# Queued weight splits, redealt product banks and a shared decay-weight buffer in a two-layer hybrid encoder

## The chip, the cores and the metric

The kernel runs on one core of a Trainium2 chip. The metric is device time in microseconds, the median of several executions. A profiled execution gives a trace of every instruction; times in the text count from the start of its span. The core's engines work side by side, each through its own instructions in order: TensorE (PE; PEld is its weight load), VectorE (DVE), ScalarE (ACT), GpSimd (POOL) and SyncE (SP), which here only issues DMAs. POOL issues DMAs as well, among them DMAs that add their source to what the destination holds.

## What is computed

The reference runs two layers over 512 tokens of width 1024. Each layer is a token mixer (first a gated DeltaNet, GDN, then gated linear attention, GLA), a residual with LayerNorm, a squared-ReLU MLP of width 4096, and a residual with LayerNorm again:

```python
for i in range(DEPTH):
    m = _mixer_gdn(x, ...) if i % 2 == 0 else _mixer_gla(x, ...)
    x = _layernorm(DEEPNORM_ALPHA * x + m, ln1_g[i], ln1_b[i])
    x = _layernorm(DEEPNORM_ALPHA * x + _sq_relu_mlp(x, mlp_w1[i], mlp_w2[i]), ln2_g[i], ln2_b[i])

def _sq_relu_mlp(h, w1, w2):
    a = jax.nn.relu(jnp.matmul(h, w1))
    return jnp.matmul(a * a, w2)

def _mixer_gla(h, w_in, gate_w2, gate_b, norm_g, w_out):
    proj = jnp.matmul(h, w_in)                      # q, k, v, r and a rank-16 gate input per direction
    gate_logit = jnp.einsum('bsnr,nrk->bnsk', gl, gate_w2) + gate_b
    log_a = jax.nn.log_sigmoid(gate_logit) / B_TAU  # decay of each key channel, two directions
    ...
```

## The kernel before

Four stages follow one another on the one core: GDN, first MLP, GLA, second MLP. All large products are done to almost fp32 accuracy out of reduced-precision operands: every matrix is **split** into a high part (`hi`, a ScalarE copy that rounds) and a low part (`lo`, what is left, usually a VectorE subtraction), and `mm3` issues three matmuls for one: hi·hi, hi·lo and lo·hi (L119 to L121). So every weight tile goes through the same steps: a DMA from HBM on SP's queue into one of **three buffers** of the tag `wst` (`Ctx.dma`, L50), the ScalarE copy (L96) and the VectorE subtraction (L101) into `wh` and `wl`, of which there are three each. `split` has another form, `by_dma`: ScalarE writes hi and the negated source (L98), and a POOL DMA adds the source to it (L99); VectorE isn't used.

The instructions are traced in the order of the Python code, which is also their priority; a scheduler then places each on its engine's queue, when its own model of time says that its data and buffers are there. A later stage's instruction may so come to stand ahead of an earlier stage's. What is once placed on an engine runs in that order. Orders that are wanted are written by hand: `in_order` chains the instructions of an engine as traced, and `issue_after(ins)` puts what is traced within it behind `ins` on the same engine.

**The MLP.** `mlp` takes the 4096 hidden features in four groups of eight tiles. Group 0's features are computed plainly (`feature`, L334 and L335 are its ReLU and square). In the later groups, `Pair` computes two feature tiles over 512 tokens with seven half-size products instead of eight (Strassen's method, 128x256 each, twelve matmuls a product), into three accumulators X, Y and Z; X and Z lie in one PSUM bank and Y in another (tag `pj`, two banks). ScalarE copies or VectorE sums read them (L448 after product 1, L451 after product 2, L454, L457, L460, L463, then the ReLUs). The order of the products is 1, 2, 6, 5, 7, 3, 4. The scheduler treats a bank as a whole: a matmul into a bank waits for the read of its other half.

The second matrix is multiplied with the same method on the level of blocks: `second` runs seven products (1, 2, 5, 6, 7, 3, 4) for each group, interleaved with the next group's `Pair` products on TensorE, and `last` does it for the last group alone. `pair` splits an operand out of the hidden features (`ah`, `al`), `load` fetches a block of the second matrix (`w2r`, eight buffers), `split(i)` splits it (`w2h`, `w2l`), `plus` adds one block to another. In `last`, the order on POOL, ScalarE and VectorE is fixed up to product 3; after that come a4's `pair`, product 7 with the sums `full` (L584), the LayerNorm `norm` of token tiles 0 and 1 (on VectorE L224, L227, L233, L195 to L202, L238; on ScalarE the squares of L226 and the Ln and Exp of L193 and L194), and product 4, into which the transposes of those tiles are put (`turn`, `xpose`, L181, with the copies L184 and L185). The LayerNorms of tiles 2 and 3 come behind it.

**The GLA stage** begins with `proj_halves`: the gates' input (`gps`), then head 0's q (`pjq`) and k (`pjk`), for the first half of the tokens and then the second, with the transposes of tiles 2 and 3 in the middle of k's first half. Its weights are traced in this order: `gst` (split by `side_by_side`, L160 and L162), q, k, and, behind `proj_halves`, the decay weights `gate_w2` of the two directions: each into its own `wst` buffer `w2f`, a ScalarE copy of 96 rows (L793) and a VectorE subtraction in 32 of them (L794). Then the gates of head 0 follow (`gates`: a matmul `lg`, L864, five ScalarE steps, a VectorE sum, L866 to L872), and the levels of the decayed scores (`levels`, `scp`, L950, each fed by VectorE products such as `qh`, L961).

`behind(n)` puts n **units** of other matmul work in front of what follows on TensorE: one token tile of a quarter of v and r's depth (`vr`, six matmuls), a quarter of a q or k projection (`qk`, six matmuls) or a piece of the output projection. There are 104 units in all, and the calls ask for 8 ahead of the first level, 24 for each of the four heads and what is left at the end.

**The MLP's beginning.** The weights of features 0 to 2 are fetched ahead by the stage before, those of features 3 to 7 in `mlp`. At feature 5 the first blocks of the second matrix, (0, 0) and (0, 1), are loaded, at feature 6 block (1, 1), and there the first block is split and a1's pair made. `x_blocks` builds the sums of x that the `Pair` products need, in four of the eight `w2r` buffers, from feature 5 on.

Of the kernel before, what the change touches and what calls it, by code (L numbers as in the profile page):

```python
# [8 lines left out]
F32 = mybir.dt.float32  # L9
# [8 lines left out]
P = 128  # L18
S = 512
# [9 lines left out]
class Ctx:  # L29
# [55 lines left out]
    def split(self, src, shape, pool=None, by_dma=False):  # L85

        nc = self.nc
        if pool is None:
            hi = self.whl.tile(shape, F32R, name="wh", tag="wh")
            lo = self.whl.tile(shape, F32R, name="wl", tag="wl")  # L90
        else:
            pool, hi, lo, bufs = pool
            if pool:
                hi = pool.tile(shape, F32R, name=hi, tag=hi, bufs=bufs)
                lo = pool.tile(shape, F32R, name=lo, tag=lo, bufs=bufs)
        nc.scalar.copy(hi, src)  # L96
        if by_dma:
            nc.scalar.mul(lo, src, -1.0)  # L98
            nc.gpsimd.dma_start(lo, src, accum_op=ALU.add)  # L99
        else:  # L100
            nc.vector.tensor_tensor(lo, src, hi.bitcast(F32), ALU.subtract)  # L101
        return hi, lo

    def wcols(self, w, c0, n=P, pool=None):

        st = self.wst.tile([P, KT, n], F32, name="wst", tag="wst")
        self.dma(st, w[:, c0:c0 + n].rearrange("(k p) n -> p k n", p=P))
        return self.split(st, [P, KT, n], pool)

# [64 lines left out]
    def xpose(self, t, src, tags=("tp",)):  # L174

        nc = self.nc
        for q in range(2):
            ps = self.bank([P, 4, P], F32, name="tp", tag=tags[(2 * t + q) % len(tags)])
            for i in range(4):
                k = 4 * q + i  # L180
                nc.tensor.transpose(ps[:, i, :], src[:, k * P:(k + 1) * P], self.ident)  # L181
            hi = self.xth[:, 4 * q:4 * q + 4, t * P:(t + 1) * P]
            lo = self.xtl[:, 4 * q:4 * q + 4, t * P:(t + 1) * P]
            last = nc.scalar.copy(hi, ps)  # L184
            self.last_lo = nc.vector.tensor_tensor(lo, ps, hi.bitcast(F32), ALU.subtract)  # L185
        return last

    def rsqrt(self, out, x, n, eps, times=None):
# [4 lines left out]
        nc.scalar.activation(y, x, AF.Ln, bias=self.bias[eps])  # L193
        nc.scalar.activation(y, y, AF.Exp, scale=-0.5)  # L194
        nc.vector.tensor_tensor(t, y, y, ALU.mult)  # L195
# [18 lines left out]
    def layernorm(self, z, out, par, last=False, sums=None):  # L214
# [21 lines left out]
        for q in range(2):  # L236
            if True:
                nc.vector.scalar_tensor_tensor(out[q], out[q], rstd[:, 0:1], par[2 + q], ALU.mult, ALU.add)  # L238
            else:
# [69 lines left out]
def mlp(c, w1, w2, g, b, out=None, extra=None):  # L309
# [14 lines left out]
    with c.banks(pj=2, X=2, Y=2, Z=2), tc.tile_pool(name="mlp", bufs=2) as pool:  # L324
# [73 lines left out]
        class Pair:  # L398
# [41 lines left out]
            def products(self, h):  # L440
# [3 lines left out]
                l, r = slice(0, HT), slice(HT, S)  # L444
                xz, y = c.bank([P, 2, HT], F32, name="fxz", tag="pj"), c.bank([P, 2, HT], F32, name="fy", tag="pj")
                X, Z, Y = xz[:, 0, :], xz[:, 1, :], y[:, 0, :]
                self.mm(X, 1)
                A.copy(h0[:, l], X)  # L448
                yield
                self.mm(Z, 2, False)  # L450
                V.tensor_tensor(h0[:, l], h0[:, l], Z, ALU.add)  # L451
# [3 lines left out]
                yield  # L455
                self.mm(Y, 5)
                A.copy(h1[:, r], Y)  # L457
# [104 lines left out]
        def last(gi, h, a):  # L562
# [82 lines left out]

# [123 lines left out]
def gla(c, gc, w_in, gate_w2, w_out, ln_g, ln_b, w_next):  # L769
# [5 lines left out]
    with c.banks(ac=2, tp=2, pj=4), tc.tile_pool(name="gla", bufs=2) as pool:  # L775
# [10 lines left out]
        R = slice(0, 32), slice(32, 64), slice(64, 96)  # L786
        glr, w2r = [], []
        for d in range(2):
            w2f = c.wst.tile([96, S], F32, name="w2f", tag="wst")
            src = gate_w2[d]  # L790
            c.dma(w2f, bass.AP(src.tensor, src.offset, [[0, 6]] + [list(q) for q in src.ap]))
            t = pool.tile([96, S], F32R, name=f"w2r{d}", bufs=1)
            nc.scalar.copy(t, w2f)  # L793
            nc.vector.tensor_tensor(t[R[2], :], w2f[R[2], :], t[R[2], :].bitcast(F32), ALU.subtract)  # L794
            w2r.append(t)
            g = pool.tile([96, S], F32R, name=f"glr{d}", bufs=1)
# [11 lines left out]
        with c.in_order(mybir.EngineType.PE):  # L808
# [13 lines left out]

            behind(8)
            after = None
# [895 lines left out]
```

## Time and profile before

| | |
|---|---|
| median of 3 executions | 1362.85 us (1362.2 to 1363.65) |
| the profiled execution | 1365.3 us |
| its span | 1363.6 us |
| mean granted clock of TensorE | 0.991 of full |
| TensorE, VectorE, ScalarE, GpSimd busy | 97%, 80%, 58%, 9% of the span |
| matmuls | 8629 |
| DMA traffic | 153.16 MB, mean 112 GB/s |

In rows of the timeline stand the start and the duration in us, the engine, the line, the operation, what is written and read with shapes, and in brackets how long the engine stood idle before and what released it. Names are tiles of the program; several instructions of one kind in a row are merged (x2). The view of waits sums, for each pair of instructions, the time that the first one's engine stood idle for the second. The chain of waits follows the work that ended last back to the start.

### The profile page before, as it was taken

Reading aid. Unit: us, or ns where it says so; the run is one execution under the profiler, and the core shown is the slowest. Engines: PE = TensorE matmul, PEld = TensorE weight load, DVE = VectorE, ACT = ScalarE, POOL = GpSimd, SP = SyncE. Lnnn points to the kernel's source line nnn. Section 1 sums busy time; section 2 is a strip of 40 time slices with the busy share of each in tenths; the row PEclk is TensorE's granted clock in tenths of the full one; section 3 lists DMA queues with packets and bytes.
Section 4 is the critical chain, followed back from the end, with each engine's and each line's share of the span. In section 5 each row is a group of like instructions: output and inputs, shape, how many; then the busy total and the mean of one; then the engine's idle time right before and its main releaser. Section 6 shows DMA issues by size and latency. Waiting matters only on the chain.

```text
span 1363.6 us, 22194 instructions
## 1 busy us (share of the span) xinstructions
PE 1328.0 (97%) x8629; PEld 1128.2 (83%) x8629; DVE 1096.5 (80%) x1786; ACT 794.6 (58%) x1552; POOL 118.4 (9%) x169
## 2 busy tenths in 40 slices
PE   8999999999999999999998999999999999999996
PEld 8777777778777989889897878888889789898985
DVE  6687877788777878989887877967879678989888
ACT  3776568665743555666566555654445456566654
POOL 4000000000000910101101100000000001101010
PEclk9999999999999999999998999999999999999998
DMA  6221112110141684775647332212225576757555
GB/s 178 76 63 48 48 32 63 47 48 32 63 135 52 189 186 141 161 182 151 150 143 155 95 119 62 78 47 74 81 78 160 144 178 146 161 167 144 153 136 127
DMA packets 155532, 153.16 MB, mean 112 GB/s; under 512 B 7659, under 2 KB 122467, under 8 KB 155427
## 3 DMA queue, kind: packets, MB, share of 16 engines
q1 hardware_dynamic: 144355, 111.90, 27.8%
q0 software_dynamic: 11072, 39.86, 15.1%
q8 instruction: 67, 1.10, 0.3%
q14 instruction: 38, 0.31, 0.1%
HBM read 113.99 MB, written 2.10 MB: 85 GB/s over the span
## 4 chain that ended last, share of the span: by engine, by line
PE 75%; DVE 12%; ACT 8%; issue 2%; DMA 2%; DVEq 0%; SPq 0%; POOL 0%; ACTq 0%; POOLq 0%
PE fxz L119 3%; PE fxz L121 3%; PE fxz L120 3%; PE pjv L119 3%; PE pjv L120 3%; PE pjv L121 3%; PE pX L119 2%; PE pX L120 2%; PE pX L121 2%; PE pY L120 2%; PE scp L950 2%; PE pY L121 2%; PE op L1646 2%; PE pY L119 2%; PE pj L121 2%
## 5 line engine op out<-in xcount | busy, mean ns | idle before, releaser
L96 ACT CAST wh<-wst 128x1024 fp32r<-128x1024 f32 x150 | 157.2, 1048 | 164.9 <-PE pjz L120 41.0
L101 DVE TENSOR_TENSOR wl<-wst,wh 128x1024 fp32r<-128x1024 f32 x150 | 184.3, 1231 | 54.3 <-ACT wh L96 53.5
L101 DVE TENSOR_TENSOR w2l<-w2r,w2h 128x1024 fp32r<-128x1024 f32 x92 | 112.5, 1223 | 33.9 <-ACT w2h L96 33.7
L96 ACT CAST w2h<-w2r 128x1024 fp32r<-128x1024 f32 x94 | 98.4, 1047 | 60.0 <-PE pX L121 24.7
L364 POOL DMA_DIRECT2D w2r<-w2r x56 | 48.3, 892 | 512.0 <-DVE w2l L101 297.1
L96 ACT CAST ah<-h 128x1024 fp32r<-128x1024 f32 x56 | 58.8, 1050 | 53.1 <-PE pZ L120 19.6
L101 DVE TENSOR_TENSOR al<-h,ah 128x1024 fp32r<-128x1024 f32 x56 | 68.4, 1222 | 8.4 <-ACT ah L96 8.4
L119 PE MATMUL fxz<-xth,wh 128*128 128x256 f32 x264 | 74.8, 283 | 0.2 <-ACT h L448 0.2
L121 PE MATMUL fxz<-xth,wl 128*128 128x256 f32 x264 | 74.5, 282 | 0.0
L120 PE MATMUL fxz<-xtl,wh 128*128 128x256 f32 x264 | 74.5, 282 | 0.0
L413 DVE TENSOR_TENSOR wst<-wst 128x512 f32<-128x512 f32 x110 | 73.1, 683 | 0.2
L119 PE MATMUL pj<-xth,wh 128*128 128x256 f32 (+1 forms) x192 | 64.8, 339 | 2.3 <-ACT xth L184 1.4
L120 PE MATMUL pX<-w2l,ah 128*128 128x512 f32 x168 | 66.1, 394 | 0.0
L119 PE MATMUL pX<-w2h,ah 128*128 128x512 f32 x168 | 66.1, 393 | 0.0
L121 PE MATMUL pX<-w2h,al 128*128 128x512 f32 x168 | 65.7, 391 | 0.0
L120 PE MATMUL pj<-xtl,wh 128*128 128x256 f32 (+1 forms) x192 | 64.7, 337 | 0.0
L121 PE MATMUL pj<-xth,wl 128*128 128x256 f32 (+1 forms) x192 | 64.6, 337 | 0.0
L119 PE MATMUL pjv<-wh,xth 128*128 128x512 f32 x128 | 54.7, 428 | 0.0
L119 PEld LDWEIGHTS fxz<-xth,wh 128*128 128x128 f32 x264 | 50.1, 190 | 4.8 <-ACT h L448 1.5
L120 PEld LDWEIGHTS fxz<-xtl,wh 128*128 128x128 f32 x264 | 50.2, 190 | 2.4
L119 PE MATMUL fxz<-xh,wh 128*128 128x256 f32 x176 | 50.2, 285 | 1.6 <-DVE h L451 1.4
L121 PE MATMUL pjv<-wh,xtl 128*128 128x512 f32 x128 | 50.2, 392 | 0.0
(504 smaller groups left out, 4256.0 us busy)
## 6 DMA issues: line engine op xcount, KB each, us to landing
wst<-in_mlp_w SPq DMA_DIRECT2D x68, 512.0 KB, 5.1
w2r<-in_mlp_w SPq DMA_DIRECT2D x60, 512.0 KB, 4.3
w2r<-w2r POOLq DMA_DIRECT2D x56, 512.0 KB, 5.7
wst<-in_a_w_in SPq DMA_DIRECT2D x32, 512.0 KB, 4.1
wst<-in_b_w_in SPq DMA_DIRECT2D x32, 256.0 KB, 3.1
wst<-in_a_w_out SPq DMA_DIRECT2D x8, 512.0 KB, 3.9
wst<-in_b_w_in SPq DMA_DIRECT2D x8, 512.0 KB, 3.9
wst<-in_b_w_out SPq DMA_DIRECT2D x8, 512.0 KB, 3.7
```

The source lines that it names most:

```text
L96: nc.scalar.copy(hi, src)
L101: nc.vector.tensor_tensor(lo, src, hi.bitcast(F32), ALU.subtract)
L119: mm(ps, ah, bh, start=start, stop=False, **kw)
L120: mm(ps, ah, bl, start=False, stop=False, **kw)
L121: mm(ps, al, bh, start=False, stop=stop, **kw)
L364: nc.gpsimd.dma_start(blocks[a + (q,)], blocks[b + (q,)], accum_op=ALU.add)
L413: plus = lambda a, b: V.tensor_tensor(a, a, b, ALU.add)
L950: T.matmul(ps[:, n, :], kh[:, sl], qh[:, sl], start=True, stop=True)
L1646: T.matmul(op[:, n, :], l, r, start=i == 0, stop=i == len(mm) - 1)
```

## The change

It has five parts.

1. `split` and the LayerNorm keep hold of some of their instructions (`halves`: the copy and the subtraction of the latest plain split; `normed`: the Exp and the last VectorE step of the latest LayerNorm). `wcols` takes a list `late` of instructions behind which its split is queued. GLA's q weights are split behind the two halves of a4's pair in the MLP's `last`, GLA's k weights behind the second LayerNorm's Exp, and k's lo is made by a POOL DMA (`by_dma`).
2. In `products`, X has a bank for itself, and Y and Z share one.
3. The two directions' decay weights are loaded into one `wst` buffer, ahead of `proj_halves` in the trace; each is split by two ScalarE operations (64 rows of hi, 32 rows negated) and a POOL DMA.
4. In both MLPs, block (0, 0) of the second matrix is loaded at feature 4, and the first block's split is queued behind the last transposes' copies (`last_hi`, `last_lo`).
5. `behind(8)` ahead of GLA's first level becomes `behind(9)`.

```diff
-        nc.scalar.copy(hi, src)
+        h = nc.scalar.copy(hi, src)
         if by_dma:
             nc.scalar.mul(lo, src, -1.0)
             nc.gpsimd.dma_start(lo, src, accum_op=ALU.add)
         else:
-            nc.vector.tensor_tensor(lo, src, hi.bitcast(F32), ALU.subtract)
+            self.halves = h, nc.vector.tensor_tensor(lo, src, hi.bitcast(F32), ALU.subtract)
...
-    def wcols(self, w, c0, n=P, pool=None):
+    def wcols(self, w, c0, n=P, pool=None, late=(), by_dma=False):
         st = self.wst.tile([P, KT, n], F32, name="wst", tag="wst")
         self.dma(st, w[:, c0:c0 + n].rearrange("(k p) n -> p k n", p=P))
-        return self.split(st, [P, KT, n], pool)
+        with contextlib.ExitStack() as es:
+            for i in late:
+                es.enter_context(self.tc.issue_after(i.ins))
+            return self.split(st, [P, KT, n], pool, by_dma)
...
-            last = nc.scalar.copy(hi, ps)
+            self.last_hi = last = nc.scalar.copy(hi, ps)
...
-        nc.scalar.activation(y, y, AF.Exp, scale=-0.5)
+        self.exped = nc.scalar.activation(y, y, AF.Exp, scale=-0.5)
...
-                nc.vector.scalar_tensor_tensor(out[q], out[q], rstd[:, 0:1], par[2 + q], ALU.mult, ALU.add)
+                self.normed = self.exped, nc.vector.scalar_tensor_tensor(out[q], out[q], rstd[:, 0:1], par[2 + q], ALU.mult, ALU.add)
...
-                xz, y = c.bank([P, 2, HT], F32, name="fxz", tag="pj"), c.bank([P, 2, HT], F32, name="fy", tag="pj")
-                X, Z, Y = xz[:, 0, :], xz[:, 1, :], y[:, 0, :]
+                x, yz = c.bank([P, 2, HT], F32, name="fx", tag="pj"), c.bank([P, 2, HT], F32, name="fyz", tag="pj")
+                X, Z, Y = x[:, 0, :], yz[:, 0, :], yz[:, 1, :]
...
-                self.mm(Z, 2, False)
+                self.mm(Z, 2)
...
-                self.mm(Y, 5)
+                self.mm(Y, 5, False)
...
             a4 = pair(a22)
+            c.late = c.halves
...
             norm(1, False)
+            second_normed = c.normed
...
-            return norm
+            return norm, second_normed
...
+            if f == 4:
+                load(0, 0, 0)
             if f == 5:
-                load(0, 0, 0)
                 load(0, 0, 1)
             if f == 6:
                 load(0, 1, 1)
-                split(1)
+                with tc.issue_after(c.last_hi.ins), tc.issue_after(c.last_lo.ins):
+                    split(1)
...
-            norm = last(G - 1, h, a)
+            norm, normed = last(G - 1, h, a)
         norm(2, False)
         norm(3, True)
+        c.normed = normed
...
-        specs += [(c.wcols(w_in, c0), nm, "pj") for c0, nm in ((0, "pjq"), (H * P, "pjk"))]
+        specs += [(c.wcols(w_in, c0, late=late, by_dma=i > 0), nm, "pj")
+                  for i, (c0, nm, late) in enumerate(((0, "pjq", c.late), (H * P, "pjk", c.normed)))]
+        R = slice(0, 32), slice(32, 64), slice(64, 96)
+        w2f = c.wst.tile([96, 2, S], F32, name="w2f", tag="wst")
+        for d in range(2):
+            src = gate_w2[d]
+            c.dma(w2f[:, d, :], bass.AP(src.tensor, src.offset, [[0, 6]] + [list(q) for q in src.ap]))
+        w2r = [pool.tile([96, S], F32R, name=f"w2r{d}", bufs=1) for d in range(2)]
         with c.in_order(mybir.EngineType.PE):
             gps, *qk0 = c.proj_halves(specs, ...)
-        glr, w2r = [], []
+        glr = []
         for d in range(2):
-            w2f = c.wst.tile([96, S], F32, name="w2f", tag="wst")
-            c.dma(w2f, ...)
-            t = pool.tile([96, S], F32R, name=f"w2r{d}", bufs=1)
-            nc.scalar.copy(t, w2f)
-            nc.vector.tensor_tensor(t[R[2], :], w2f[R[2], :], t[R[2], :].bitcast(F32), ALU.subtract)
+            nc.scalar.copy(w2r[d][0:64, :], w2f[0:64, d, :])
+            nc.scalar.mul(w2r[d][R[2], :], w2f[R[2], d, :], -1.0)
+            nc.gpsimd.dma_start(w2r[d][R[2], :], w2f[R[2], d, :], accum_op=ALU.add)
+        for d in range(2):
...
-            behind(8)
+            behind(9)
```

More of the change, by code (lines that the diff above doesn't have):

```diff
@@ L782, in gla @@
         specs = [(c.side_by_side(gst, 32), "gps", "ac")]
-        specs += [(c.wcols(w_in, c0), nm, "pj") for c0, nm in ((0, "pjq"), (H * P, "pjk"))]
+        specs += [(c.wcols(w_in, c0, late=late, by_dma=i > 0), nm, "pj")
[6 more added lines that the diff above has]
+        w2r = [pool.tile([96, S], F32R, name=f"w2r{d}", bufs=1) for d in range(2)]
         with c.in_order(mybir.EngineType.PE):
             gps, *qk0 = c.proj_halves(specs, at={(0, 2, 4 * j): lambda t=2 + j: c.xpose(t, c.xt[t], ("tp", "pj")) for j in range(2)})
-        R = slice(0, 32), slice(32, 64), slice(64, 96)
-        glr, w2r = [], []
+        glr = []
         for d in range(2):
-            w2f = c.wst.tile([96, S], F32, name="w2f", tag="wst")
-            src = gate_w2[d]
-            c.dma(w2f, bass.AP(src.tensor, src.offset, [[0, 6]] + [list(q) for q in src.ap]))
-            t = pool.tile([96, S], F32R, name=f"w2r{d}", bufs=1)
-            nc.scalar.copy(t, w2f)
-            nc.vector.tensor_tensor(t[R[2], :], w2f[R[2], :], t[R[2], :].bitcast(F32), ALU.subtract)
-            w2r.append(t)
+            nc.scalar.copy(w2r[d][0:64, :], w2f[0:64, d, :])
+            nc.scalar.mul(w2r[d][R[2], :], w2f[R[2], d, :], -1.0)
+            nc.gpsimd.dma_start(w2r[d][R[2], :], w2f[R[2], d, :], accum_op=ALU.add)
+        for d in range(2):
             g = pool.tile([96, S], F32R, name=f"glr{d}", bufs=1)
```

## The prediction

> **What bounds the kernel now.** First the page's head:
>
> ```profile
> span 1363.6 us, 22194 instructions
> PE 1328.0 (97%) x8629; PEld 1128.2 (83%) x8629; DVE 1096.5 (80%) x1786; ACT 794.6 (58%) x1552; POOL 118.4 (9%) x169
> ```
>
> TensorE is busy for 97% of the span, so a change that neither adds nor removes a matmul can win only from the 35.6 us in which it is not, and from time in which its clock is low. The view of waits, for TensorE alone, says what it waits for; these are its lines that the diff can touch (waited for: us in total, times, longest).
>
> ```profile
> PE pY L120 <- DVE w2l L101: 2.8, 3, 1.7
> PE scp L950 <- DVE qh L961: 2.2, 2, 1.5
> PE pY L119 <- ACT w2h L96: 1.4, 1, 1.4
> PE fxz L119 <- DVE h L451: 1.4, 2, 0.7
> PE tp L181 <- DVE xt L238: 1.1, 1, 1.1
> PE pj L119 <- ACT h L334: 1.0, 1, 1.0
> PE fxz L119 <- ACT h L448: 0.2, 1, 0.2
> ```
>
> Together 10.1 us. The largest, pY, lies in the first MLP's last products. ScalarE's timeline there (start, us, instruction, idle before it and its releaser):
>
> ```profile
> 724.86 1.05 ACT L96 CAST wh<-wst 128x1024 fp32r<-128x1024 f32 x1 [6.77 <-DMA wst<-in_b_w_in]
> 725.81 1.04 ACT L96 CAST ah<-h 128x1024 fp32r<-128x1024 f32 x1
> 726.76 1.04 ACT L96 CAST w2h<-w2r 128x1024 fp32r<-128x1024 f32 x1
> ```
>
> The cast at 724.86 is not the MLP's: it splits the GLA stage's q weights. It stands on ScalarE ahead of the MLP's own ah and w2h, and ScalarE stood still for 6.77 us until q's transfer landed. The MLP's splits then came in a heap, and TensorE stopped twice (1.4 and 1.7 above, 3.1 together). The windows there show a second cost (window, us, then busy PE, PEld, DVE, ACT, POOL, then granted clock, DMA share, GB/s):
>
> ```profile
> 728.00:731.00 3.00, 1.26 (x3) 0.85 (x4) 3.00 (x3) 3.00 (x4) 0.67 (x1) 0.70 0.62 175
> 731.00:734.00 3.00, 3.00 (x8) 2.32 (x8) 3.00 (x4) 1.53 (x2) 1.02 (x2) 0.50 0.86 169
> 734.00:737.00 3.00, 3.00 (x10) 2.36 (x9) 2.91 (x4) 0.00 (x0) 0.85 (x1) 0.66 0.95 186
> 737.00:740.00 3.00, 3.00 (x15) 2.46 (x15) 0.72 (x1) 1.81 (x2) 0.85 (x1) 1.00 1.01 197
> ```
>
> After the stop the clock is at 0.50: 8 matmuls in 3 us where 15 fit, and it is whole again only near 737.
>
> **Part 1: the splits of q and k queued behind the MLP's.** The stop's price can be read without a model, since the second MLP runs the same products with no stage behind it. Two points of the chain of waits, in both MLPs (start, us):
>
> ```profile
> 647.22 1.14 DVE w2l L101
> 747.29 1.30 DVE xt L584 x4
> 1238.68 1.13 DVE w2l L101
> 1332.88 1.30 DVE xt L584 x4
> ```
>
> From point to point the first MLP takes 100.07 us, the second 94.20. With q's split behind a4's, its weights are long there when ScalarE gets to it, and the first MLP should run like the second: **-5.87**. The least it can be is the stop alone, -3.1; I take the twin's value, because it holds the slow clock too.
>
> [...]
>
> q's split does not vanish. Its half on VectorE lay in an idle stretch and comes to a full one:
>
> ```profile
> 725.94 1.22 DVE L101 TENSOR_TENSOR wl<-wst,wh 128x1024 fp32r<-128x1024 f32 x1 [4.73 <-ACT wh L96]
> 756.21 1.22 DVE L101 TENSOR_TENSOR al<-h,ah 128x1024 fp32r<-128x1024 f32 x1
> 757.35 0.34 DVE L224 SCALAR_TENSOR_TENSOR bmv<-lns,bias 128x1 f32<-128x1 f32 x2
> 758.07 0.69 DVE L584 SCALAR_TENSOR_TENSOR xt<-pX,xt 128x512 f32<-128x512 f32 x1 [0.38 <-PE pX L121]
> 763.53 1.32 PE L181 MATMUL tp<-ident,xt 128*128 128x128 f32 x8
> ```
>
> 756.21 is a4's lo, behind which q's lo is now queued. Right after it starts the first LayerNorm, at whose end TensorE takes the transposes of 763.53. VectorE's only hole is the 0.38 at 758.07, and everything queued behind q's lo (sums, LayerNorms, transposes' lo) waits 1.22 less what fits in holes. Bounds 0 and +1.22; I take **+1.1**, near the upper one, since the hole is small. q's hi on ScalarE (1.05) lies behind a4's ah, where ScalarE waits for the LayerNorm: nothing.
>
> k's split leaves VectorE: a copy and a multiplication on ScalarE (1.05 each) and a POOL DMA that adds the source. Both are queued behind the second LayerNorm's Exp.
>
> ```profile
> 762.06 0.20 ACT L194 ACTIVATE rsy<-rsy 128x1 f32<-128x1 f32 x1
> 751.88 0.86 POOL L99 DMA_DIRECT2D xl<-wst  x1 [1.04 <-ACT xl L98]
> 777.79 1.13 POOL L210 DMA_DIRECT2D ln<-in_ln_g  x2 [25.05 <-PE tp L181]
> w2r<-w2r POOLq DMA_DIRECT2D x56, 512.0 KB, 5.7
> 775.69 0.36 PE L119 MATMUL pjk<-xth,wh 128*128 128x256 f32 x1
> ```
>
> In the clock of this trace: 762.26 + 2 x 1.05 = 764.4 on ScalarE, 0.86 to issue, 5.7 to land: 771.0. pjk's third matmul needs it at about 776, so it is covered by 5 us. ScalarE's next work (the copies of the transposes begun at 763.53) is delayed by some 0.1 us. POOL has nothing between 751.88 and 777.79. Cost: nothing, and if the cover goes, rival A.
>
> [...]
>
> **Part 2: w2f in one buffer, its lo by DMA, one more unit before the levels.** The GLA stage's first stop is scp, 2.2 us (1.5 and 0.7). What it waits for:
>
> ```profile
> 777.97 0.68 DVE L794 TENSOR_TENSOR w2r<-w2f,w2r 32x512 fp32r<-32x512 f32 x1
> 787.36 1.05 ACT L96 CAST wh<-wst 128x1024 fp32r<-128x1024 f32 x1 [1.79 <-DMA wst<-in_b_w_in]
> 787.07 0.63 PE L864 MATMUL lg<-glr,w2r 96*128 96x512 f32 x2
> 798.60 0.63 ACT L872 ACTIVATE F<-gr 128x512 f32<-128x512 f32 x1 [1.36 <-DVE gr L871]
> ```
>
> TensorE gives the gates' logits at 787.07, but ScalarE stands 1.79 us for v's weights, whose buffers the two w2f tiles held till 778 (777.97 reads one). The gate chain ends at 798.60, and the scores wait for it. In the new kernel w2f holds one of the three buffers, so v's second transfer starts when k's buffer comes free (771.0 by the sum above) and not after 778.6. And behind(9) puts six more matmuls ahead of the scores: 15 start in 3.00 us above, so at least 1.2 us, taken from no other place, since the units only move up by one. 1.79 + 1.2 covers 2.2: **-2.2**; bounds -1.2 (the unit alone) and -2.2. w2f's split takes ScalarE four operations for two and two POOL DMAs more (0.86 each, ahead of the ln loads), against two of 0.68 less on VectorE; from 778 to 787 there is room: nothing.
>
> **Part 3: half-size products' banks.** Today product 2 waits for the copy of product 1 (L448) and product 6 for VectorE's sum (L451), because X and Z share a bank. After it X is alone, and Y, who now shares with Z, comes one product and one chunk later. Removed: 1.4 + 0.2 = **-1.6**. Bounds 0 and -1.6; between product 2 and product 5 lie product 6 (twelve half-size matmuls) and a chunk (six full ones), some 1.2 us each at 15 full ones in 3.00, and L451's sum is late by no more than 0.7 today, so I take all of it.
>
> **Part 4: block (0, 0) one feature sooner.** Its two 512 KB transfers pass feature 5's weights on SP's queue. The stop this can touch is pj's 1.0, in the second MLP:
>
> ```profile
> 1035.02 9.65 SPq L50 DMA_DIRECT2D w2r<-in_mlp_w  x5
> 1045.07 1.04 ACT L96 CAST wh<-wst 128x1024 fp32r<-128x1024 f32 x1
> 1053.72 11.12 DMA w2r<-in_mlp_w
> 1064.86 1.05 ACT L96 CAST w2h<-w2r 128x1024 fp32r<-128x1024 f32 x1 [7.31 <-DMA w2r<-in_mlp_w]
> ```
>
> ScalarE waits 7.31 us for a block whose transfer took 11.12 in a crowd. The earlier block thins the crowd, by how much no row tells: 0 to -1.0, and I take **-0.5**. Should the block's buffer be no sooner free than at 1035.02, feature 5's weights wait behind it till then and still have 10 us to the cast of 1045.07. The order of its split behind the transposes costs nothing; it runs behind them today.
>
> **Sum.** -5.87 + 1.1 - 2.2 - 1.6 - 0.5 = -9.1 us. The profiled execution took 1365.3 us, 1.7 more than its span and 2.45 more than the median of 1362.85; so 1356.2 for it, and **1353.8 for the median**.
>
> **Rivals.**
>
> A, k's lo comes late. Two transfers in a row must land: k's weights, whose buffer comes free only when the MLP's last blocks let go of it (near 755, after the POOL DMAs issued up to 751.88), and the POOL DMA. With the slowest weights quoted, 11.12 us, for both: 755 + 11.1 + 2.1 + 0.9 + 11.1 = 780.2, 4.2 past need, and a stop of over 3 us brings the slow clock with it (2.8): -9.1 + 7.0 = -2.1, **1360.8**. For it: today q's weights kept ScalarE waiting 6.77 us. Against it: the median of 5.7.
>
> B, ScalarE's wait moves into the GLA stage. w2f's one buffer comes free only after its POOL DMAs, v's third weights are late, and ScalarE stands for them ahead of the gates. If it stands as long as it does today in the MLP, 6.77 for 1.79, the gates lose 5.0 against the 1.2 of the added unit: part 2 turns from -2.2 into +3.8, and 2.8 of slow clock come on top: -9.1 + 6.0 + 2.8 = -0.3, **1362.6**. Against it: v's second weights start some 7 us sooner, so one transfer instead of two is in flight by then.
>
> C, slower. POOL works in order. Should k's DMA stand behind the two pairs of ln loads, the first of which begins at 777.79 after 25.05 us of waiting, it issues at 777.79 + 2 x 1.13 = 780.1 and lands 0.86 + 5.7 later, at 786.6: 10.6 past need, 2.8 of slow clock, so -9.1 + 13.4 = +4.3, **1367.1**. It decides once the DMA is 6.3 us past need. Against it: k's DMA is traced ahead of those loads and its data are there 13 us before them.
>
> D, the change does not do what it says: another GLA instruction takes the q split's place on ScalarE, which still stands. Parts 2 to 4 alone are left, -4.3, **1358.6**. Against it: the stage's splits that the diff queues behind nothing run before the stop or after the last LayerNorm:
>
> ```profile
> 713.95 0.50 ACT L160 CAST wh<-gst 128x128 fp32r<-128x128 f32 x2 [1.67 <-PE fy L120]
> 776.82 1.14 ACT L793 CAST w2r<-w2f 96x512 fp32r<-96x512 f32 x2 [0.27 <-DVE xt L238]
> ```
>
> **How the numbers follow.** Forecast 0.66, A 0.09, B 0.09, C 0.08, D 0.08. The forecast's own range: at best -5.87 - 2.2 - 1.6 - 1.0, and the 1.1 of xt L238 too should VectorE lose nothing to q's lo: -11.8, 1351.1; at worst -3.1 + 1.22 - 1.2, 1359.8. The range to be given goes from 1350.3, for waits too short for that view, to 1360.8; it takes in D and half of A and leaves out B and C. A measurement of this kernel can tell about 0.2%, 2.7 us, from no change. Faster: the forecast, D and the lesser degrees of A and B, 0.66 + 0.08 + 0.08 = 0.82; the same, the rest of A and B, 0.10; slower, C, 0.08.
>
> **What would show it.** ScalarE's 6.77 us gone and the clock at 1.00 from 720 to 740; the first MLP's stretch near 94 us; q's lo behind a4's; k's DMA landing before pjk; no wait of scp, nor of fxz for L451. Wrong if pjk waits for its lo, or the sum of TensorE's waits is no smaller.

## The result and the profile after

The changed kernel takes **1351.85 us** (median of 6 runs, 1350.98 to 1353.9) against 1362.73 (6 runs, 1361.13 to 1363.65) for the kernel before: **10.9 us less**, ratio 0.9922 with a 95% interval of 0.9909 to 0.9934, which is 9.0 to 12.4 us. The prediction was 9.1 us less, 1353.8. The total is near; three of the prediction's four parts are not, as shown below.

The page's head after:

```profile
span 1350.2 us, 22201 instructions
PE 1320.3 (98%) x8629; PEld 1125.8 (83%) x8629; DVE 1092.9 (81%) x1783; ACT 797.7 (59%) x1555; POOL 121.2 (9%) x172
```

TensorE's waits after, the lines that answer to those of before:

```profile
PE scp L961 <- DVE qh L972: 1.5, 2, 0.9
PE pY L123 <- DVE w2l L101: 1.4, 2, 0.7
PE tp L184 <- DVE xt L241: 1.0, 1, 1.0
PE stp L1031 <- ACT kdt L1021: 0.4, 1, 0.4
PE pX L122 <- ACT rsy L197: 0.3, 1, 0.3
```

pY has lost half of its wait and its ScalarE partner, fxz and the pj behind h are gone. scp has only gone from 2.2 to 1.5, and the last two lines, 0.7 together, are new. By these lines alone the change would be worth 5.5 us (10.1 before, 4.6 after); the time says twice that. So the trace was also cut into stretches, from the start of one named matmul to the start of another. Such a stretch holds every wait and every slow clock in it, whatever the view of waits makes of them. In us, the kernel before as it is and all others as their difference to it:

```
                 start   MLP 1    MLP 1   gates    GLA     MLP 2   MLP 2
                         middle   last                     first   middle
before           433.70  204.34   47.11   13.87    210.40  71.83   204.73
after             -2.53   -2.30   -6.01   +0.64     -0.07  -1.30    -1.93
a1_after_again    -3.53   -2.30   -6.05   +0.64     -0.93  -1.29    -1.93
e1_early_splits   -0.95   -2.30   -2.03   +0.01     -0.59  -1.29    -1.93
e10_early_again   -0.16   -2.30   -0.17   +0.02     -0.44  -1.29    -1.93
e2_old_banks      +0.65   -0.19   -6.01   +0.64     -1.35  -1.30    +0.04
e3_late_block     -0.66   -2.30   -6.01   +0.62     -1.08  +0.68    -1.93
e4_old_w2f_8      -2.05   -2.30   -6.01   +0.62     +0.10  -1.30    -1.93
e7_old_w2f        +0.45   -2.30   -6.05   +0.61     -1.02  -1.29    -1.93
e8_behind8        +0.90   -2.30   -6.05   +0.61     -0.27  -1.30    -1.93
e5_v_queued       -1.12   -2.30   -6.05   +0.63     -2.35  -1.30    -1.93
e6_both_queued    -2.04   -2.30   -6.01   +0.62     -2.72  -1.28    -1.93
e11_both_again    -1.50   -2.30   -6.07   +0.61     -2.72  -1.29    -1.93
e9_q_by_dma       -0.40   -2.30   -6.04   +0.24     -2.70  -1.29    -1.93
```

*start*: to the first product of the first MLP's first weights (pj). *MLP middle*: from the first matmul into pY to the 144th, the half-size products and the groups between. *MLP 1 last*: from there to the last matmul into pY. *gates*: on to the first gps. *GLA*: from the gates' logits (lg) to the first output projection (ob). *MLP 2 first*: from that MLP's first pj to its first pY. What is left over is the same in all to 0.17 us.

Two things can be read at once. The columns of the MLPs repeat to 0.07 us from profile to profile of the same code, so a difference of 0.5 us is safe in them, where a time is only good to about 2.7. There is one exception: e1 and e10 are the same code and differ by 1.86 in *MLP 1 last*, which is taken up below. And the *start* differs by 4.4 us from one profile to another although the same instructions run there in all of them; the last section shows what it goes with. The 2.53 us by which the changed kernel's profile is better there are not the change's. Without them the changed kernel's own profile has lost 10.9 us.

What became of the stop. The granted clock and the counts in windows of 3 us after (us; busy PE, PEld, DVE, ACT, POOL; clock, DMA share, GB/s):

```profile
722.00:725.00 3.00, 3.00 (x15) 2.47 (x14) 2.42 (x3) 2.45 (x3) 0.56 (x1) 1.00 1.10 214
725.00:728.00 3.00, 3.00 (x15) 2.49 (x14) 3.00 (x4) 0.68 (x1) 0.85 (x1) 1.00 0.96 190
728.00:731.00 3.00, 3.00 (x15) 2.49 (x14) 3.00 (x4) 3.00 (x4) 0.85 (x1) 1.00 0.96 187
```

Fifteen matmuls in each, at clock 1.00. In the kernel before the three windows from 725 to 734 us held 8, 3 and 8; the prediction shows the second and the third, and this is the first:

```profile
725.00:728.00 3.00, 1.62 (x8) 0.99 (x6) 2.06 (x3) 3.00 (x4) 0.00 (x0) 1.00 0.00 0
```

With the second (1.26) TensorE was busy for 2.88 of 6 us there.

VectorE's timeline at the place to which q's lo went:

```profile
745.37 1.23 DVE L101 TENSOR_TENSOR al<-h,ah 128x1024 fp32r<-128x1024 f32 x1
746.51 0.35 DVE L227 SCALAR_TENSOR_TENSOR bmv<-lns,bias 128x1 f32<-128x1 f32 x2
746.77 1.22 DVE L101 TENSOR_TENSOR wl<-wst,wh 128x1024 fp32r<-128x1024 f32 x1
747.91 0.75 DVE L236 SCALAR_TENSOR_TENSOR xt<-xt,bmv,ln 128x512 f32<-128x512 f32 x1
```

It runs behind a4's lo (745.37) and the first means, and the LayerNorm's next step (747.91) waits for it. The hole of 0.38 us that stood there before is filled, and the *gates* stretch is 0.64 longer. k's two halves, ScalarE's timeline and then POOL's:

```profile
751.35 1.03 ACT L96 CAST wh<-wst 128x1024 fp32r<-128x1024 f32 x1
752.29 1.05 ACT L98 ACTIVATE wl<-wst 128x1024 fp32r<-128x1024 f32 x1
```

```profile
753.93 0.86 POOL L99 DMA_DIRECT2D wl<-wst  x1 [12.05 <-ACT wl L98]
767.55 1.13 POOL L213 DMA_DIRECT2D ln<-in_ln_g  x2 [12.77 <-DVE xtl L188]
768.65 0.90 POOL L805 DMA_DIRECT2D w2r<-w2f  x1
770.55 0.79 POOL L805 DMA_DIRECT2D w2r<-w2f  x1 [0.41 <-ACT w2r L804]
```

k's DMA is issued 13.6 us ahead of the ln loads, right after its multiplication, and is 5.2 us on its way; pjk's third matmul, which needs it, starts at 765.79, 6.6 us after it has landed. TensorE's view of waits has no line of pjk. w2f's DMAs are another matter. The second is issued at 770.55, when ScalarE's multiplication for it is done, and is 4.9 us on its way (the first took 3.9). Until then w2f's buffer is held. What SyncE's queue waited for from 750 to 790 us, its next issues and ScalarE's timeline show what follows:

```profile
SPq L50 <- DMA w2r<-w2f: 15.4, 1, 15.4
SPq L50 <- DMA wl<-wst: 9.6, 1, 9.6
```

```profile
775.61 2.42 SPq L50 DMA_DIRECT2D wst<-in_b_w_in  x5
```

```profile
779.30 1.05 ACT L96 CAST wh<-wst 128x1024 fp32r<-128x1024 f32 x1 [3.00 <-DMA wst<-in_b_w_in]
780.25 0.58 ACT L907 COPY k<-pjk 128x512 f32<-128x512 f32 x1
780.73 0.69 ACT L877 ACTIVATE ge<-lg,gb 128x512 f32<-128x512 f32 x1
```

The wait of 9.6 ends when k's DMA has landed, and v's second weights leave at 759.21; in the kernel before they left at 778.68. The wait of 15.4 ends when w2f's second DMA has landed: only then, at 775.61, v's third weights are issued, the first of five transfers in a row. ScalarE stands 3.00 us for them at 779.30, ahead of k's copy and of the gates at 780.73. Before, it stood 1.79 us for v's second weights and 0.41 for the third, 2.20 together. That is rival B, in a mild form.

### The profile page after: what moved, and what is told of

Read it like the earlier page. It is cut to its first block, busy times and chain, and to the rows that moved or that the text cites. A ratio compares the mean times of both kernels' runs of the same rounds, so it can differ in the third digit from the quotient of the medians.

```text
span 1350.2 us, 22201 instructions
## 1 busy us (share of the span) xinstructions
PE 1320.3 (98%) x8629; PEld 1125.8 (83%) x8629; DVE 1092.9 (81%) x1783; ACT 797.7 (59%) x1555; POOL 121.2 (9%) x172
## 4 chain that ended last, share of the span: by engine, by line
PE 79%; DVE 9%; ACT 8%; issue 2%; DMA 1%; DVEq 0%; SPq 0%; ACTq 0%
PE fx L124 3%; PE fx L123 3%; PE fx L122 3%; PE pX L123 3%; PE pX L122 3%; PE pX L124 3%; PE pjv L122 3%; PE pj L124 3%; PE pj L122 3%; PE pj L123 3%; PE pjv L123 3%; PE pjv L124 2%; PE fyz L124 2%; PE fyz L122 2%; PE fyz L123 2%
## 5 line engine op out<-in xcount | busy, mean ns | idle before, releaser
L123 PE MATMUL pjv<-wl,xth 128*128 128x512 f32 x128 | 50.0, 390 | 0.0
L124 PE MATMUL fx<-xh,wl 128*128 128x256 f32 x176 | 49.7, 283 | 0.0
L124 PE MATMUL fyz<-xh,wl 128*128 128x256 f32 x176 | 49.7, 282 | 0.0
L124 PE MATMUL fx<-xth,wl 128*128 128x256 f32 x176 | 49.7, 282 | 0.0
L123 PE MATMUL fx<-xtl,wh 128*128 128x256 f32 x176 | 49.7, 282 | 0.0
L122 PE MATMUL fyz<-xh,wh 128*128 128x256 f32 x176 | 49.7, 282 | 0.0
```

The source lines that it names most:

```text
L122: mm(ps, ah, bh, start=start, stop=False, **kw)
L123: mm(ps, ah, bl, start=False, stop=False, **kw)
L124: mm(ps, al, bh, start=False, stop=stop, **kw)
```

## The experiments

Each kernel is the changed one with the edits named, timed beside the kernel before on the same chip. On the three chips used here the kernel before took 1363.53, 1365.13 and 1365.19 us, so ratios are compared, and stretches.

### Without the queueing of q's and k's splits

```diff
-  specs += [(c.wcols(w_in, c0, late=late, by_dma=i > 0), nm, "pj") ...
+  specs += [(c.wcols(w_in, c0), nm, "pj") ...
```

> The changed kernel, but GLA's q and k weights are split as before (queued behind nothing, both low parts on VectorE); the rest of the change stays. Theory 1 (the first MLP's gain is the ScalarE wait for q's transfer, with the slow clock behind it): ScalarE stands some 6 to 7 us again ahead of the MLP's last splits, the granted clock falls to about 0.5 for some us, and the time goes up by 6.4 less the 1.0 that q's low part costs VectorE now, so by about 5.4 us, to 1357.2. Rival (the gain comes from the other parts, the twin comparison of the two MLPs is a coincidence): no such wait, and the time stays within 1.5 us of 1351.9. Rival 2 (the stop alone without the clock): 1351.9 + 3.1 - 1.0 = 1354.

> The kernel with q's and k's splits where they were (the rest of the change kept), once more. ScalarE will stand near 6.7 us for q's weights again and TensorE some 4 to 5 us behind it. The question is the clock after the stop: 0.50 in the kernel before, 1.00 in the first run of this kernel. If the clock falls by chance, or with the phase of some window, it may fall this time, and the first MLP's last stretch comes out near 47.1 us; if this kernel's stop never lowers it, the stretch is 45.1 us again. The ratio to the kernel before should be 0.9956 once more.

1359.55 us, ratio 0.9956 (0.9943 to 0.9969); and once more 1358.16, 0.9959 (0.9947 to 0.9972). So about 0.35%, near 4.8 us, of the gain goes with this part. ScalarE's line for q's weights is there again in both, e1 first, then e10:

```profile
721.57 1.05 ACT L96 CAST wh<-wst 128x1024 fp32r<-128x1024 f32 x1 [6.74 <-DMA wst<-in_b_w_in]
```

```profile
722.22 1.05 ACT L96 CAST wh<-wst 128x1024 fp32r<-128x1024 f32 x1 [6.62 <-DMA wst<-in_b_w_in]
```

The windows behind it differ, though the code is the same. The first run, for which the slow clock was expected:

```profile
722.00:725.00 3.00, 1.65 (x7) 0.82 (x5) 2.34 (x3) 3.00 (x4) 0.00 (x0) 1.00 0.00 1
725.00:728.00 3.00, 1.26 (x6) 1.00 (x6) 3.00 (x4) 3.00 (x4) 0.85 (x1) 1.00 0.64 179
728.00:731.00 3.00, 3.00 (x15) 2.46 (x14) 3.00 (x3) 1.25 (x2) 0.85 (x1) 1.00 0.89 171
```

The second run of the same code:

```profile
722.00:725.00 3.00, 1.98 (x9) 1.27 (x7) 1.70 (x2) 2.78 (x3) 0.00 (x0) 1.00 0.00 0
725.00:728.00 3.00, 1.05 (x2) 0.69 (x3) 3.00 (x4) 3.00 (x5) 0.31 (x1) 0.75 0.63 175
728.00:731.00 3.00, 3.00 (x8) 2.30 (x7) 3.00 (x4) 1.90 (x3) 1.39 (x2) 0.50 0.72 143
731.00:734.00 3.00, 3.00 (x10) 2.35 (x9) 3.00 (x4) 0.00 (x0) 0.85 (x1) 0.61 1.07 209
```

TensorE is busy 2.91 of the first 6 us in the one (1.65 + 1.26), and 3.03 in the other, and its two waits for pY there are 1.3 and 1.7 us in the one, 1.2 and 1.7 in the other: much the same stop. Behind it the clock stays at 1.00 in the one, with 15 matmuls in 3 us, and falls to 0.50 in the other, with 8. The *MLP 1 last* stretch tells the price: 45.09 against 46.95, where the changed kernel has 41.11. The stop alone costs 4.0 us, and the slow clock, when it comes, 1.9 more.

### The banks as before

```diff
-  x, yz = c.bank(...), c.bank(...)      # X alone, Z and Y share
+  xz, y = c.bank(...), c.bank(...)      # X and Z share, Y alone
-  self.mm(Z, 2)            self.mm(Y, 5, False)
+  self.mm(Z, 2, False)     self.mm(Y, 5)
```

> The changed kernel with the half-size products' banks dealt as before (X with Z, Y alone). Theory 1 (what the banks cost stands in the weight loads' waits, 3.4 us in the first MLP and 3.0 in the second, of which 2.3 and 1.9 came back with the change): the time goes up by 4.2 us, to 1356.0, spread over all groups of the half-size products. Rival (only the waits of the matmuls themselves count, 1.6 us, as the prediction summed): 1353.5, and the stages' ends move by 0.7 and 0.7.

1357.89 us, 0.9943 (0.9931 to 0.9956), 0.2% of the time back. That lies between the two theories and within the interval of both. The stretches decide: 2.11 us come back in the first MLP's middle and 1.97 in the second's, 4.1 in all, and nothing anywhere else in the MLPs. The prediction had counted TensorE's matmul waits on that bank. The wait is also, and mostly, in front of the weight loads that stand ahead of those matmuls. The view of waits for TensorE's weight loads, in the first MLP's middle of the kernel before:

```profile
PEld fxz L119 <- DVE h L451: 2.3, 4, 1.1
PEld fxz L119 <- ACT h L448: 0.8, 2, 0.6
PEld fxz L119 <- ACT h L469: 0.3, 1, 0.3
```

and in the second MLP's:

```profile
PEld fxz L119 <- DVE h L451: 2.1, 4, 1.1
PEld fxz L119 <- ACT h L448: 0.6, 2, 0.4
PEld fxz L119 <- ACT h L469: 0.3, 1, 0.3
```

3.4 and 3.0 us. In the changed kernel this view is empty in both places; with the old banks it is back, at 3.2 and 3.1. Not all of a weight load's wait reaches the matmuls behind it: the stretches give 2.30 and 1.93.

### The block one feature later again

```diff
-  if f == 4:
-      load(0, 0, 0)
   if f == 5:
+      load(0, 0, 0)
       load(0, 0, 1)
   if f == 6:
       load(0, 1, 1)
-      with tc.issue_after(c.last_hi.ins), tc.issue_after(c.last_lo.ins):
-          split(1)
+      split(1)
```

> The changed kernel with block (0, 0) loaded at feature 5 and its split queued behind nothing, as before. Theory 1 (the earlier block took the second MLP's wait at its start away): the 1.0 us wait of pj for ScalarE comes back at the second MLP's start and the time goes up by 1.3 us, to 1353.2, all of it there. Rival (the wait went away because the stages before changed, not for this part): within 0.5 us of 1351.9 and no such wait.

1354.07 us, 0.9923 (0.991 to 0.9937): by the time alone, nothing. The stretch at the second MLP's start is 1.98 us longer than in the changed kernel, and TensorE's waits show the one that came back:

```profile
PE pj L122 <- ACT h L337: 1.7, 1, 1.7
```

It was 1.0 before. In the first MLP nothing changes. The weight loads' view has it too, in the kernel before:

```profile
PEld pj L119 <- ACT h L334: 1.4, 1, 1.4
```

and none of it in the changed one. So this part is worth 1.3 us against the kernel before, and 2.0 beside the rest of the change. The run takes back the place of the load and the order of the split together; which of the two does it stays open.

### The decay weights and the unit

Three kernels, which take back w2f's single buffer with its POOL DMAs, the ninth unit, or both:

```diff
-  w2f = c.wst.tile([96, 2, S], ...)           # one buffer, loaded early
-  nc.scalar.copy(...); nc.scalar.mul(...); nc.gpsimd.dma_start(..., accum_op=ALU.add)
+  w2f = c.wst.tile([96, S], ...)              # one for each direction
+  nc.scalar.copy(t, w2f); nc.vector.tensor_tensor(...)
-  behind(9)
+  behind(8)
```

> The changed kernel with the decay weights as before (two buffers, loaded behind the projections, low part on VectorE) and 8 units ahead of the first level. Theory 1 (this part won nothing: the buffers that the weights of v wait for now come free when the POOL DMAs have landed, so ScalarE stands longer than before, 3.0 for 2.2 us, and the added unit only makes up for it): within 0.7 us of 1351.9, the wait of scp near 2.2 again and the gates' first ScalarE step 0.7 us sooner after the logits. Rival (as predicted, the part is worth 2.2 us): 1354.1.

> The changed kernel with the decay weights as before (two buffers, behind the projections, low part on VectorE), but 9 units ahead of the first level. Theory 1 (one buffer that is freed by POOL DMAs delays v's third weights by 0.8 us against two that VectorE frees): ScalarE stands about 2.2 us in place of 3.0, scp's wait shrinks by 0.7 from 1.5 to about 0.8 or less, 1351.2. Rival (the single buffer is right and the unit did nothing): 1351.9 or slower, with scp's wait of 1.5 or more.

> The changed kernel with 8 units ahead of the first level. Theory 1 (the unit covers 1.36 us of scp's wait and is taken from nowhere): scp waits 1.36 us more, about 2.9, and the time is 1353.2; if the unit is also what makes stp wait 0.4, that goes and it is 1352.5. Rival (the scores' pace is set by VectorE, so the unit only moves the wait): within 0.4 us of 1351.9.

Old w2f and eight units 1352.96 us, 0.9916 (0.9902 to 0.9929); old w2f alone 1354.17, 0.9918 (0.9904 to 0.9931); eight units alone 1354.85, 0.9921 (0.9908 to 0.9935). None differs from the changed kernel by more than its interval. The *GLA* column separates them. The changed kernel's GLA code ran in six profiles (after, a1, e1, e10, e2, e3), and gave -0.07 to -1.35. The spread goes with ScalarE's stop for v's third weights, and with TensorE's wait for scp behind it. The lines of the banks' experiment, ScalarE first, then TensorE's waits:

```profile
783.69 1.05 ACT L96 CAST wh<-wst 128x1024 fp32r<-128x1024 f32 x1 [2.12 <-DMA wst<-in_b_w_in]
```

```profile
PE scp L961 <- DVE qh L972: 0.7, 1, 0.7
```

And of the changed kernel with eight units:

```profile
781.78 1.05 ACT L96 CAST wh<-wst 128x1024 fp32r<-128x1024 f32 x1 [2.09 <-DMA wst<-in_b_w_in]
```

```profile
PE scp L961 <- DVE qh L972: 2.0, 2, 1.3
```

In the six profiles with nine units ScalarE's stop and scp's wait are 2.12 and 0.7, 2.36 and 0.9, 2.37 and 0.9, 2.68 and 1.2, 2.94 and 1.4, 3.00 and 1.5. The wait is the stop less about 1.5, each time. With eight units it is the stop less 0.1. So the ninth unit is worth 1.3 to 1.4 us of that wait, and 1.1 of the stretch: at like stops, -1.35 against -0.27 (2.12 and 2.09), and -1.02 against +0.10 with the old w2f (2.28 and 2.39). The 2.9 us of scp that were expected with eight units would have needed a stop of 3.0; this execution's was shorter.

The single buffer does not take the stop away, and the old buffers with nine units do not either. There ScalarE stands for v's second weights, and 0.19 us more for the third, 2.28 together:

```profile
780.38 1.06 ACT L96 CAST wh<-wst 128x1024 fp32r<-128x1024 f32 x1 [2.09 <-DMA wst<-in_b_w_in]
```

So what the single buffer changes is the cause of the stop: two weights' transfers at once before (issued at 778.68 and 780.76, 7.4 us to landing in the median of the six DMAs from 777 to 786 us, where the changed kernel's took 3.0 from 757 to 785), the landing of w2f's second DMA after. How long that DMA is on its way goes with the stretch. In the six profiles it takes 4.9, 4.6, 4.5, 4.2, 4.2 and 4.0 us, and *GLA* reads -0.07, -0.59, -0.44, -0.93, -1.08 and -1.35. Against the one profile of the old buffers (-1.02) the single buffer is worth 0.3 us in the best case and costs 1.0 in the worst.

### The changed kernel again, on another chip

> The changed kernel itself, on the chip and in the call of the two runs that are compared with it. Theory: the gain is the change's, so its ratio to the kernel before is 0.992 here too (0.9909 to 0.9934 in the first comparison). From the program's start to the first product of the MLP's first weights the profiles differ by up to 3.4 us for the same code, and the GLA stage from its gates' logits to its last head by up to 1.3 us; both should be elsewhere within those again, while the MLPs' stretches should come out the same to 0.05 us. If the stretches of the MLPs move too, the readings by stages are worth less than taken.

1353.75 us, 0.9923 (0.9909 to 0.9937), beside a kernel before of 1363.53. The ratio repeats, and so do the stretches of the MLPs, to 0.05 us.

### The waits of ScalarE queued away

If v's third weights are rival B's stop, then the device of part 1 should cure it: queue those splits behind the gates' last step on ScalarE. A second edit queues the next MLP's first splits behind head 3's last kdt copy, since ScalarE stands for these too. The changed kernel's timeline:

```profile
973.63 1.05 ACT L96 CAST wh<-wst 128x1024 fp32r<-128x1024 f32 x1 [1.83 <-DMA wst<-in_mlp_w]
974.58 0.58 ACT L1021 COPY kdt<-kdp 128x512 f32<-128x512 f32 x1
```

1.83 us ahead of the kdt copy, for which TensorE waits 0.4 (the stp line above).

```diff
   # e5: the third and fourth split of head 0's v
+  with contextlib.ExitStack() as es:
+      if h == 0 and q > 1:
+          es.enter_context(c.tc.issue_after((self.first_gated if q == 2 else self.gated).ins))
-  wh, wl = c.split(st, [P, 2, 2 * B_DV])
+      wh, wl = c.split(st, [P, 2, 2 * B_DV])
   # e6, e11: that, and
-  ahead=lambda: c.take_ahead(w_next, 3)
+  ahead=lambda: c.take_ahead(w_next, 3, (c.kdt,))
```

> The changed kernel, and head 0's third and fourth split of the v weights queued behind the gates' last ScalarE step of the first and of the second direction. Theory 1 (scp waits because ScalarE stands 3.0 us for v's third weights ahead of the gates): the gates start some 3 us sooner after the logits, scp's wait of 1.5 us is gone, and the time is 1351.9 - 1.5 = 1350.4. Rival (the gates are late for another reason, VectorE's or the logits'): the wait of ScalarE moves and scp waits as long as now, 1351.9. Rival 2: the v splits come too late for the units, pjv waits, and the time is above 1352.5.

> As the run before, and the splits of the second MLP's first three weights queued behind head 3's last copy of the transposed keys. Theory 1 (the stop of stp, 0.4 us with 0.3 of weight load, is ScalarE standing 1.8 us for the next MLP's weights ahead of that copy): that wait is gone and the time is 0.7 us below the run before, 1349.7. Rival: the order shifts the wait to another transfer, no gain.

> The kernel with both waits of ScalarE queued away, once more, beside the changed kernel on the same chip. Theory: v's third weights cost the GLA stage about 1.5 us and the next MLP's weights 0.2 to 0.4, so its time is 1.5 to 2 us below that of the changed kernel in this call, and its ratio to the kernel before is near 0.990. Rival: the difference seen so far (0.9896 against 0.9922 in another call) is spread between calls, and the two come out alike here.

v's splits alone 1351.99 us, 0.9903 (0.989 to 0.9917); both 1350.24, 0.9896 (0.9882 to 0.9909), and on another chip 1350.34, 0.9909 (0.9894 to 0.9924), where the changed kernel has 1353.75. The times put both some 0.15 to 0.25% ahead of the changed kernel, about what they can tell; the *GLA* column does not leave it open. It is -2.35 with v's splits queued, and -2.72 with both, twice. ScalarE's timeline with v's splits queued:

```profile
776.65 1.04 ACT L96 CAST wh<-wst 128x1024 fp32r<-128x1024 f32 x1
778.45 0.59 ACT L909 COPY k<-pjk 128x512 f32<-128x512 f32 x1 [0.76 <-PE pjk L124]
778.94 0.69 ACT L878 ACTIVATE ge<-lg,gb 128x512 f32<-128x512 f32 x1
```

No split stands between 776.65 and k's copy now; ScalarE waits for TensorE's pjk, not for a DMA, and no wait for scp is left in that kernel's view of waits. TensorE's matmuls do not wait for kdt in any of the three kernels, but that alone says nothing: they do not in the changed kernel's second profile either, where ScalarE's stop ahead of the copy was 1.59 us. The weight loads tell them apart. With v's splits alone they still wait:

```profile
PEld stp L1036 <- ACT kdt L1026: 0.5, 1, 0.5
```

With both edits that line is gone, in both profiles. The second edit is worth 0.37 us (-2.35 to -2.72), where 0.7 was expected.

### q's lo by DMA too

```diff
-  by_dma=i > 0
+  by_dma=True
```

> The kernel with both waits of ScalarE queued away, and q's lo made as k's is: a copy and a multiplication on ScalarE and a POOL DMA that adds the source, so VectorE has no q split behind a4's. Theory: q's lo on VectorE is what takes 0.64 us between the first MLP's last product of the Y bank and the gates' first product; that stretch falls back from 14.5 to 13.87 us, and the time by some 0.6 us against the run with both waits queued away (0.9896), to about 0.989. Rival: ScalarE's extra 1.05 us stands ahead of the first LayerNorm's squares and takes as much back, so the stretch stays at 14.5. Second rival: q's lo lands after its product wants it, TensorE waits for pjq and the kernel is slower.

On top of both queuings: 1349.77 us, 0.9898 (0.9884 to 0.9912), 0.6 us below e11 on the same chip, which the intervals cannot tell apart. The *gates* stretch falls from 14.48 to 14.10, not to 13.87. VectorE has its hole back, and ScalarE has lost one:

```profile
748.59 0.34 DVE L227 SCALAR_TENSOR_TENSOR bmv<-lns,bias 128x1 f32<-128x1 f32 x2
749.31 0.69 DVE L587 SCALAR_TENSOR_TENSOR xt<-pX,xt 128x512 f32<-128x512 f32 x1 [0.38 <-PE pX L124]
```

```profile
748.28 1.05 ACT L98 ACTIVATE wl<-wst 128x1024 fp32r<-128x1024 f32 x1
749.23 0.71 ACT L229 ACTIVATE xh<-xt,bmv 128x512 f32<-128x512 f32 x1
```

The LayerNorm's squares start at 749.23, straight behind the added multiplication and 0.64 us behind the means' start (748.59); before they started 0.25 behind it. So 0.4 of the 0.64 comes back and the rival takes the rest. This kernel's median is the lowest here, but its ratio is not below e6's 0.9896, and e11's interval does not let it be called faster.

## Why the prediction was right, and where it was not

Term by term, in us; "measured" is from the stretches:

```
                                  predicted   measured
q's and k's splits queued           -5.87      -6.01
q's lo on VectorE                   +1.1       +0.64
w2f in one buffer, ninth unit       -2.2       -0.07 (six profiles: -0.07 to -1.35)
banks                               -1.6       -4.23
block one feature sooner            -0.5       -1.30
sum                                 -9.1      -10.97
```

**Part 1 was right, and for its reason.** The first MLP's last stretch now takes 41.11 us, the second's same stretch 41.02: the twin comparison held to a tenth. The stop went and the clock stayed at 1.00; e1 and e10 bring the stop back, and e10 the slow clock. One qualification comes from these two: 1.9 of the 6.01 us are clock that falls in some executions and not in others, so the kernel before, of which there is one profile, need not always be as slow there as in it. By the time, the part is worth some 4.8 us, between the stop's 4.0 less 0.64 and the full 6.01 less 0.64.

The clock behind like stops was not the same. TensorE's two waits for pY are 1.4 and 1.7 us in the kernel before, 1.3 and 1.7 in e1, 1.2 and 1.7 in e10; the clock behind them is 0.50, 1.00 and 0.50, and e1 and e10 are the same code. What decides it, no run shows. The prediction counted the slow clock into the stop's price after one profile; it was right about the kernel before and too sure about the next execution. The 2.8 us of slow clock in the rivals' sums, 5.87 less the stop's 3.1, were the author's estimate, which no run shows; the runs showed 1.9 where the clock fell (e10 against e1) and nothing where it did not.

**q's lo was over-sized.** The prediction took +1.1, because the hole on VectorE was small. Start to start the operation takes 1.14 us (746.77 to 747.91), and the hole of 0.38 takes a third of it. That leaves 0.76, which the rows quoted gave; 0.64 was measured, and the last 0.1 is not explained.

**k's lo behind POOL** was covered, as it said: issued at 753.93, long before the ln loads. Rivals A and C fell with that, and rival D with the splits' place behind a4's and behind the Exp.

**Part 2 failed in one step**: that the 1.79 go because "v's second transfer starts when k's buffer comes free". That transfer did start then (759.21). But ScalarE then stands for the third weights in its place, because w2f's buffer is now let go only when its second POOL DMA has landed: issued at 770.55, 4.9 us on its way, and the next transfers leave at 775.61. The prediction had costed the issue of the two DMAs (0.86 each) and set it against room on the engines; it had not added their flight to the time for which the buffer is held, and had that only as rival B. ScalarE's stop went from 2.20 to between 2.1 and 3.0 us instead of to nothing. The other half, "at least 1.2 us" for the unit, was nearly right: 1.1. Rival B's sign was right and its size, a stop of 6.77 with the slow clock behind it, was far too large. That ScalarE's stop makes scp wait, e5 shows by removing it; that w2f's DMA holds the third weights back, the queue's wait of 15.4 us shows.

**Part 3 was mis-sized**: 1.6 for 4.23. The mechanism was right, and the view was too narrow. Only the matmuls' waits were summed, and the list quoted holds no weight loads. The loads' waits, 3.4 and 3.0 us, were in the profile of before, in the same view for the other queue of TensorE.

**Part 4 was mis-sized** too: 0.5 taken, 1.3 measured, above its bound of 1.0. The wait is gone altogether, so the upper end was the nearer one, and that end was read from the matmuls again: the weight load waited 1.4.

So the sum came out near in part by luck: parts 3 and 4 gave 2.6 and 0.8 us more than was taken and q's lo cost 0.5 less, while part 2 gave 2.1 less in the changed kernel's profile, 0.9 to 2.1 over the six.

## What to carry to other kernels

A split for the next stage, put into an engine's queue before its data had landed, stopped what was queued behind it here: q's held ScalarE for 6.77 us, ahead of the MLP's ah and w2h. So look for the longest "idle before, released by a DMA" on that engine, and queue the operation behind the last one that does not need it. When a change moves such a buffer to be released by a DMA, ask at once who is next in the buffer's ring: here the stop came up again there, 3.00 us for v's third weights. To size a wait on TensorE, read its weight loads' waits as well as its matmuls' (here 3.4 and 3.0 us at the banks, where the matmuls' own came to 1.6 in both MLPs together), and check the sum against stretches between named matmuls.

## What the runs showed of the hardware

The clock behind one and the same stop is not fixed. Three profiles have ScalarE's stop of 6.6 to 6.8 us with TensorE busy for 2.88 (before), 2.91 (e1) and 3.03 (e10) of the 6 us behind it; the clock fell to 0.50 in the first and the last and stayed at 1.00 in e1. The fall cost 1.9 us (46.95 in e10 against 45.09 in e1).

The clock also sorts the program's start, which holds the same instructions in all fourteen profiles and took between 430.17 and 434.60 us. In four profiles the windows from 6 to 45 us show 1.00 throughout, and the start takes 430.17 to 431.66 us. In four others the clock falls to half near 40 us (in e1 0.97, 0.50 and 0.96 in the windows from 36 to 45), and it takes 432.20 to 433.04. In the other six it falls near 10 us as well (in the kernel before 0.50 and 0.94 in the windows from 9 to 15, then 0.62 and 0.81 in those from 39 to 45), and it takes 433.30 to 434.60. So the starts of single profiles differed by 4.4 us for nothing that a change did, and the granted clock told where.
